# Two weight sums by accumulating transfers, deeper load-ahead, and one more seven-product block in an encoder layer

## The chip, the cores and the metric

The kernel runs on one core of a Trainium2 chip. The metric is device microseconds of one execution; the median of three runs before the change is 883.03 us (882.75 to 883.29). TensorE (PE) multiplies, VectorE (DVE) and ScalarE (ACT) do elementwise work, GpSimd (POOL) does nearly nothing, SyncE (SP) issues nearly all transfers. All arithmetic is float32; each matrix product is made of three TensorE passes over a high and a low part of both operands, so every weight block is first split into two tiles.

## The reference

An encoder layer over 528 tokens (16 learned ones and 512 given) of width 1024: a feed-forward part, a mixer, a second feed-forward part, a last norm. Each feed-forward part is

```
gate, up = split(rms_norm(h) @ w_in)      # 1024 -> 2 x 2816
h = h + 0.5 * (silu(gate) * up) @ w_out   # 2816 -> 1024
```

The mixer runs a gated linear recurrence in both directions on half of the width and a two-dimensional Fourier transform in groups on the other half, norms both, and projects back to 1024. The output drops the first 16 tokens.

## The kernel before

Activations lie feature by partition: 8 tiles of 128 features by 528 (first layer) or 512 tokens (second). The 2816 hidden features are 22 blocks f of 128. For each block the gate and the up projection are needed, each with 8 weight tiles of 128 x 128.

A classic block (`project`, L454) makes gate and up one after the other: 8 weight tiles times three passes times, in the first layer, two halves of 264 tokens, so 48 matmuls for each and 96 for both. A pair block (`pair`, L376) treats gate and up, two halves of the 8 weight tiles and two halves of the tokens as a 2 x 2 by 2 x 2 product and makes seven products of quarter size in place of eight, 7 x 4 x 3 = 84 matmuls of 264 columns (256 in the second layer). It needs sums of weight quarters (`pair_blocks`, `pair_sums`, `pair_differences`, L96 to L128: four VectorE additions in place on the two raw tiles of 512 KB) and sums of quarters of the activations (`sums_of_x`, L289, once per layer, tiles `z` and `xg` with one buffer each, split into `th` and `tl`). In the first layer blocks 0 to 3 are classic (`CLASSIC1`, L28), in the second 0 and 1; all others are pairs.

Blocks go in chunks; the output projection of a chunk ("out" steps, eight per chunk) is interleaved with the next chunk's blocks (`ffn_steps`, L145). The last two products of a pair are made inside the next pair (`interleaved`, L425), then come the activation function and the split of the result (L409 to L421).

Every weight block is a job in one list (`jobs`). A pair is three jobs. `block` (L217) takes the next job and prepares up to `LOOK` = 3 further ones: it loads the raw tile (ring `wraw`, 4 buffers of 512 KB, SP's queue) and splits it by a ScalarE copy and a VectorE subtraction (L87 and L88, L211 and L212) into a ring of 5 pairs of tiles (`wsp`). A load waits until its buffer of the ring is free, and SP issues in order.

Each engine has one queue in order. Its order is written by a list scheduler when the program is built, by the order of the code and by what it holds ready, so an instruction can stand ahead of one that the code has earlier. PSUM has 8 banks in one ring (L72). In the first layer the first three projections (`lead`, L523) hold two banks each until block 0 and 1 are evacuated by `gate_up` (L444), whose tiles `q` and `u` have two buffers each.

Of the kernel before, what the change touches and what calls it, by code (L numbers as in the profile page):

```python
# [9 lines left out]
F32 = mybir.dt.float32  # L10
F32R = mybir.dt.float32r
AF = mybir.ActivationFunctionType
ALU = mybir.AluOpType
# [13 lines left out]
CHUNKS2 = [4, 5, 5, 4, 4]  # L27
CLASSIC1 = {0, 1, 2, 3}  # L28
CLASSIC2 = {0, 1}
# [28 lines left out]

LOOK = 3


@with_exitstack
def encoder_layer(ctx: ExitStack, tc: tile.TileContext, xT, vecs, w1i, w1o, wm, wg, wo, w2i, w2o,
# [29 lines left out]
    def quarter(t, i):  # L93
        return t[:, 512 * i:512 * (i + 1)].rearrange("p (k m) -> p k m", m=P)

    def pair_blocks(pair):  # L96

        raw = []
        for src in pair["src"]:
            r = wraw.tile([P, 1024], F32, tag="raw", name="raw")  # L100
            nc.sync.dma_start(r.rearrange("p (k m) -> p k m", m=P), src)
            raw.append(r)
        pair["raw"] = raw
        hi, lo = w_tiles()
        split_w(hi, lo, raw[0])
        jh = state["pool"].tile([P, 512], F32R, tag="jh", name="jh")
        jl = state["pool"].tile([P, 512], F32R, tag="jl", name="jl")
        split_w(jh, jl, raw[1][:, 512:])
        g, u = raw
        nc.vector.tensor_tensor(g[:, :512], g[:, :512], u[:, :512], op=ALU.subtract)  # L110
        nc.vector.tensor_tensor(u[:, :512], u[:, :512], u[:, 512:], op=ALU.add)
        nc.vector.tensor_tensor(u[:, 512:], u[:, 512:], g[:, :512], op=ALU.subtract)
        return [(quarter(hi, 0), quarter(lo, 0)), (quarter(hi, 1), quarter(lo, 1)), (quarter(jh, 0), quarter(jl, 0))]

    def pair_sums(pair):

        g, u = pair["raw"]
        hi, lo = w_tiles()
        split_w(hi, lo, u)
        nc.vector.tensor_tensor(g[:, 512:], g[:, 512:], u[:, 512:], op=ALU.subtract)  # L120
        return [(quarter(hi, 0), quarter(lo, 0)), (quarter(hi, 1), quarter(lo, 1))]

    def pair_differences(pair):

        g = pair.pop("raw")[0]
        hi, lo = w_tiles()
        split_w(hi, lo, g)
        return [(quarter(hi, 0), quarter(lo, 0)), (quarter(hi, 1), quarter(lo, 1))]  # L128
# [30 lines left out]
    def ffn_jobs(wi, wo_, steps, classic):  # L159
        for kind, f, d in steps:  # L160
            if kind == "out":
                jobs.append((wo_[d][:, f[0]:f[1], :], P, f[1] - f[0], P, 8))
            elif f in classic:
                for b in range(2):
                    jobs.append((wi[f, b], P, 8, P, 2 if len(jobs) < 3 else 8))
            else:
                pair = {"src": (wi[f, 0], wi[f, 1])}
                for part in (pair_blocks, pair_sums, pair_differences):
                    jobs.append((part, pair))
# [14 lines left out]
    ready = {}  # L184
    state = {"load": 0, "next": 0, "use": 0}
    raws = {}

    def load(i):
# [3 lines left out]
        for k in range(0, n, per):  # L192
            e = min(n, k + per)
            yield nc.sync.dma_start(raw[:p, k * m: e * m].rearrange("p (n m) -> p n m", m=m), src[:, k:e, :])

    def prep(i, dest=None):
        if len(jobs[i]) == 2:
            ready[i] = jobs[i][0](jobs[i][1])
            return
        src, p, n, m, per = jobs[i]  # L200
        if i not in raws:
            for _ in load(i):
                pass
# [49 lines left out]
    def vec(name, i=0):  # L253
        return V[:, VOFF[name] + i: VOFF[name] + i + 1]

    hall = xs.tile([P, ND, T], F32, tag="h", name="hall")
    h = [hall[:, d, :] for d in range(ND)]
# [30 lines left out]

    def sums_of_x(g, t0, n, k):  # L289
        m = n // 2  # L290
        a, b = h[k][:, t0:t0 + n], h[k + 4][:, t0:t0 + n]
        xg = tmp.tile([P, HT], F32, tag="xg", bufs=1, name="xg")
        z = tmp.tile([P, 4, HT], F32, tag="z", bufs=1, name="z")
        t1, t2, t3, t4 = [z[:, i, :m] for i in range(4)]
        nc.scalar.activation(xg[:, :m], a[:, :m], AF.Copy, scale=vec(g, k))
        nc.vector.scalar_tensor_tensor(t1, a[:, m:], vec(g, k), xg[:, :m], op0=ALU.mult, op1=ALU.subtract)
        nc.vector.scalar_tensor_tensor(t2, b[:, m:], vec(g, k + 4), t1, op0=ALU.mult, op1=ALU.subtract)
        nc.vector.tensor_tensor(t3, t2, xg[:, :m], op=ALU.subtract)
        nc.vector.scalar_tensor_tensor(t4, b[:, :m], vec(g, k + 4), t2, op0=ALU.mult, op1=ALU.subtract)
        th = xs.tile([P, 8 * QT], F32R, tag=f"th{k}", name=f"th{k}")[:, :4 * HT].rearrange("p (i t) -> p i t", i=4)  # L300
        tl = xs.tile([P, 4, HT], F32R, tag=f"tl{k}", name=f"tl{k}")
        split_to(th[:, :, :m], tl[:, :, :m], z[:, :, :m])
        return th, tl
# [45 lines left out]

    def ffn(X, XT, ss, t0, n, steps, classic, on_done, tail, lead=None):  # L350
        st = {"R": ss} if lead else {}
        half = n // 2
        with tc.tile_pool(name="ffn", bufs=10) as fp, tc.tile_pool(name="ffnt", bufs=2) as ft:
            state["pool"] = ft

            def activated(u):
# [19 lines left out]
            def pair(f, R):  # L376
# [4 lines left out]
                add = ALU.add  # L381
                q = ft.tile([P, 3, HT], F32, tag="q", name="q")
                u = ft.tile([P, 2, HT], F32, tag="u", name="u")
                q0, q1, q2 = [q[:, i, :half] for i in range(3)]
                u0, u1 = [u[:, i, :half] for i in range(2)]
                a11, a12, a22 = block()
# [24 lines left out]
                Rv = like2(R)  # L411
                gv, uv = q[:, :2, :half], u[:, :, :half]
# [49 lines left out]
            for kind, f, d in steps:  # L462
# [20 lines left out]
                else:  # L483
# [50 lines left out]
    for g in preps:  # L534
        next(g, None)
    state["next"] = state["use"] = 3
    W3 = [ready.pop(i) for i in range(3)]
    XT = []
    for k in range(ND):
# [6 lines left out]
    R = rstd_of(q, "r1")  # L546
    for k in range(4):
        XT.append(sums_of_x("g1", 0, T, k))

    ss = new_ss()  # L550
# [5 lines left out]

    ffn(X, XT, R, 0, T, STEPS1, CLASSIC1, done1, None, lead)

# [17 lines left out]

    X2, XT2 = [], []
    ss2 = new_ss()
# [266 lines left out]

    for k in range(4):
        XT2.append(sums_of_x("g2", META, SEQ, k))


    def tail(acts, ft):  # L850
# [21 lines left out]
        def group(t0, t1, between):  # L872
# [24 lines left out]
            for d in (ND - 2, ND - 1):  # L897
                ps = bank("pt")[:, :n]
                project_out(ps, d, t0, t1)
                sq = ft.tile([P, 1, 256], F32, tag="u", name="sqd")[:, :, :n]  # L900
                residual(d, d + 1, t0, t1, ps[:, None, :], sq)
# [37 lines left out]

    ffn(X2, XT2, ss2, META, SEQ, STEPS2, CLASSIC2, None, tail)  # L940

# [82 lines left out]
```

## Time and profile before

| | |
|---|---|
| median of the runs | 883.03 us |
| the profiled execution | 882.88 us |
| its span, first to last instruction | 881.1 us |
| PE busy | 867.3 us (98%), 6410 matmuls |
| DVE busy | 705.7 us (80%) |
| ACT busy | 452.6 us (51%) |
| POOL busy | 0.2 us |
| DMA | 88.14 MB, 100 GB/s in the mean |

The profiled execution's own time is 1.8 us over its span; those lie before the first and after the last instruction shown. Busy shares are means over stages: the first feed-forward layer runs from about 5 to 368 us, the mixer to about 522, the second layer and the output to the end.

### The profile page before, as it was taken

Reading aid. Unit: us, or ns where it says so; the run is one execution under the profiler, and the core shown is the slowest. Engines: PE = TensorE matmul, PEld = TensorE weight load, DVE = VectorE, ACT = ScalarE, POOL = GpSimd, SP = SyncE. Lnnn points to the kernel's source line nnn. Section 1 sums busy time; section 2 is a strip of 40 time slices with the busy share of each in tenths; the row PEclk is TensorE's granted clock in tenths of the full one; section 3 lists DMA queues with packets and bytes.
Section 4 is the critical chain, followed back from the end, with each engine's and each line's share of the span. In section 5 each row is a group of like instructions: output and inputs, shape, how many; then the busy total and the mean of one; then the engine's idle time right before and its main releaser. Section 6 shows DMA issues by size and latency. Waiting matters only on the chain.

```text
span 881.1 us, 15747 instructions
## 1 busy us (share of the span) xinstructions
PE 867.3 (98%) x6410; PEld 826.1 (94%) x6410; DVE 705.7 (80%) x1166; ACT 452.6 (51%) x701; POOL 0.2 (0%) x4
## 2 busy tenths in 40 slices
PE   9999999999999999999989999999999999999996
PEld 8999999999999999999877888999999999989996
DVE  7998776887878876967997689888787887778754
ACT  8744344444444444667837555455454444444444
POOL 0000000000000000000000000000000000000000
PEclk9999999999999999999999999999999999999998
DMA  7422332233243233423323221232433414414212
GB/s 240 151 83 87 110 107 85 85 102 115 73 121 96 76 106 106 137 78 102 118 69 96 87 81 48 84 120 85 126 102 91 128 56 140 114 48 133 73 48 96
DMA packets 33496, 88.14 MB, mean 100 GB/s; under 512 B 3728, under 2 KB 7568, under 8 KB 33424
## 3 DMA queue, kind: packets, MB, share of 16 engines
q1 hardware_dynamic: 32880, 86.62, 32.9%
q8 instruction: 50, 0.82, 0.4%
q10 hardware_dynamic: 544, 0.52, 0.2%
q14 instruction: 22, 0.18, 0.1%
HBM read 85.03 MB, written 2.10 MB: 99 GB/s over the span
## 4 chain that ended last, share of the span: by engine, by line
PE 90%; DVE 5%; ACT 2%; DMA 1%; issue 1%; SPq 1%; DVEq 0%
PE pp L233 15%; PE pp L229 14%; PE pp L231 14%; PE po L231 9%; PE po L233 9%; PE po L229 9%; PE pw L231 2%; PE pw L233 2%; PE pw L229 2%; PE pm L233 1%; PE pm L229 1%; PE pm L231 1%; PE pu L229 1%; PE pu L231 1%; PE pu L233 1%; DMA hall<-in_xT 1%
## 5 line engine op out<-in xcount | busy, mean ns | idle before, releaser
L87 ACT ACTIVATE whi<-raw 128x1024 fp32r<-128x1024 f32 x114 | 120.4, 1061 | 81.9 <-PE po L231 28.1
L88 DVE TENSOR_TENSOR wlo<-raw,whi 128x1024 fp32r<-128x1024 f32 x114 | 139.0, 1222 | 18.1 <-ACT whi L87 17.9
L211 ACT ACTIVATE whi<-raw 128x512 fp32r<-128x512 f32 (+4 forms) x120 | 88.0, 740 | 117.3 <-PE po L231 63.5
L233 PE MATMUL pp<-xh,wlo 128*128 128x256 f32 (+1 forms) x456 | 129.2, 283 | 0.0
L229 PE MATMUL pp<-th,whi 128*128 128x256 f32 (+1 forms) x456 | 129.2, 283 | 0.0
L233 PE MATMUL pp<-th,wlo 128*128 128x256 f32 (+1 forms) x456 | 129.1, 283 | 0.0
L231 PE MATMUL pp<-tl,whi 128*128 128x256 f32 (+1 forms) x456 | 129.0, 283 | 0.0
L231 PE MATMUL pp<-xl,whi 128*128 128x256 f32 (+1 forms) x456 | 128.7, 282 | 0.0
L229 PE MATMUL pp<-xh,whi 128*128 128x256 f32 (+1 forms) x456 | 128.7, 282 | 0.0
L233 PE MATMUL po<-ah,wlo 128*128 128x264 f32 (+1 forms) x496 | 128.5, 317 | 0.0
L231 PE MATMUL po<-al,whi 128*128 128x264 f32 (+1 forms) x496 | 128.5, 317 | 0.0
L229 PE MATMUL po<-ah,whi 128*128 128x264 f32 (+1 forms) x496 | 128.4, 317 | 0.0
L212 DVE TENSOR_TENSOR wlo<-raw,whi 128x512 fp32r<-128x512 f32 (+4 forms) x120 | 98.3, 824 | 10.9 <-ACT whi L211 9.3
L233 PEld LDWEIGHTS po<-ah,wlo 128*128 128x128 f32 x496 | 81.6, 188 | 6.3
L231 PEld LDWEIGHTS po<-al,whi 128*128 128x128 f32 x496 | 81.7, 188 | 5.8
L229 PEld LDWEIGHTS po<-ah,whi 128*128 128x128 f32 x496 | 81.5, 188 | 5.8 <-ACT ah L275 0.2
L229 PEld LDWEIGHTS pp<-xh,whi 128*128 128x128 f32 x456 | 86.0, 189 | 0.9
L231 PEld LDWEIGHTS pp<-xl,whi 128*128 128x128 f32 x456 | 85.8, 188 | 0.9
L233 PEld LDWEIGHTS pp<-th,wlo 128*128 128x128 f32 x456 | 86.0, 189 | 0.0
L229 PEld LDWEIGHTS pp<-th,whi 128*128 128x128 f32 x456 | 85.9, 188 | 0.0
L233 PEld LDWEIGHTS pp<-xh,wlo 128*128 128x128 f32 x456 | 85.8, 188 | 0.0
L231 PEld LDWEIGHTS pp<-tl,whi 128*128 128x128 f32 x456 | 85.8, 188 | 0.0
(218 smaller groups left out, 1736.8 us busy)
## 6 DMA issues: line engine op xcount, KB each, us to landing
raw<-in_w2i SPq DMA_DIRECT2D x44, 512.0 KB, 3.6
raw<-in_w1i SPq DMA_DIRECT2D x41, 512.0 KB, 3.8
raw<-in_w1o SPq DMA_DIRECT2D x32, 256.0 KB, 2.7
raw<-in_wm SPq DMA_DIRECT2D x12, 512.0 KB, 3.8
raw<-in_w2o SPq DMA_DIRECT2D x24, 256.0 KB, 3.0
raw<-in_w2o SPq DMA_DIRECT2D x16, 320.0 KB, 3.1
raw<-in_wo SPq DMA_DIRECT2D x8, 512.0 KB, 3.6
raw<-in_w1o SPq DMA_DIRECT2D x8, 384.0 KB, 3.2
```

The costliest lines, as they stand in the source:

```text
L87: nc.scalar.activation(hi, raw, AF.Copy)
L88: nc.vector.tensor_tensor(lo, raw, hi.bitcast(F32), op=ALU.subtract)
L211: nc.scalar.activation(hi[:p, s], raw[:p, s], AF.Copy)
L212: nc.vector.tensor_tensor(lo[:p, s], raw[:p, s], hi[:p, s].bitcast(F32), op=ALU.subtract)
L229: nc.tensor.matmul(o, wh, xh[i], start=first, stop=False, skip_group_check=go_on)
L231: nc.tensor.matmul(o, wh, xl[i], start=False, stop=False, skip_group_check=go_on)
L233: nc.tensor.matmul(o, wl, xh[i], start=False, stop=last, skip_group_check=go_on)
```

## The change

For each pair three raw buffers are loaded by SP: all of up (a), all of gate (b), and once more the first half of up (c). Two transfers issued by GpSimd then add gate's second half onto b's first half and gate's first half onto c's first half. Two VectorE additions make the other two sums. The names swap: what was gate is now up, and the activations' sums come with their signs turned (a tile `minus` of negated gains), so the gate leaves the products negated and is multiplied by -1 inside the activation function. The order at a pair's end changes with it: now gate takes the last product.

Loads are fetched up to `FETCH` = 6 jobs ahead (splits stay at 3), from a ring of 7 raw buffers in place of 4. `sums_of_x` moves into the feed-forward part and takes its scratch tile from the ring `q` (two buffers, now five quarters wide) that `gate_up` and `pair` use too; `z`, `xg` and `u` go. Block 3 of the first layer becomes a pair. The descriptor scratch of the build goes from 2048 to 1024 bytes.

```diff
-CLASSIC1 = {0, 1, 2, 3}
+CLASSIC1 = {0, 1, 2}
+FETCH = 6
-    wraw = ctx.enter_context(tc.tile_pool(name="wraw", bufs=4))
+    wraw = ctx.enter_context(tc.tile_pool(name="wraw", bufs=7))
+    def pair_loads(pair):
+        up, gate = pair["src"]
+        raw = [wraw.tile([P, 1024], F32, tag="raw", name="raw") for _ in range(3)]
+        a, b, c = [r.rearrange("p (k m) -> p k m", m=P) for r in raw]
+        nc.sync.dma_start(a, up)
+        nc.sync.dma_start(b, gate)
+        nc.sync.dma_start(c[:, :4], up[:, :4])
+        nc.gpsimd.dma_start(b[:, :4], gate[:, 4:], accum_op=ALU.add)
+        nc.gpsimd.dma_start(c[:, :4], gate[:, :4], accum_op=ALU.add)
+        pair["raw"] = raw
     def pair_blocks(pair):
-        split_w(hi, lo, raw[0])
+        split_w(hi, lo, a)
...
-        split_w(jh, jl, raw[1][:, 512:])
-        g, u = raw
-        nc.vector.tensor_tensor(g[:, :512], g[:, :512], u[:, :512], op=ALU.subtract)
-        nc.vector.tensor_tensor(u[:, :512], u[:, :512], u[:, 512:], op=ALU.add)
-        nc.vector.tensor_tensor(u[:, 512:], u[:, 512:], g[:, :512], op=ALU.subtract)
+        split_w(jh, jl, b[:, 512:])
+        nc.vector.tensor_tensor(b[:, 512:], b[:, 512:], c[:, :512], op=ALU.add)
+        nc.vector.tensor_tensor(c[:, 512:], a[:, 512:], b[:, 512:], op=ALU.add)
     def pair_sums(pair):
-        nc.vector.tensor_tensor(g[:, 512:], g[:, 512:], u[:, 512:], op=ALU.subtract)
...
+    def fetch(i):
+        if len(jobs[i]) > 2:
+            if i not in raws:
+                for _ in load(i):
+                    pass
+        elif jobs[i][0] is pair_blocks:
+            pair_loads(jobs[i][1])
     def block(dest=None):
         while state["next"] < min(len(jobs), i + LOOK + 1):
+            while state["fetched"] < min(len(jobs), i + FETCH + 1):
+                fetch(state["fetched"])
+                state["fetched"] += 1
...
-    def sums_of_x(g, t0, n, k):
+    def sums_of_x(pool, g, t0, n, k):
-        xg = tmp.tile([P, HT], F32, tag="xg", bufs=1, name="xg")
-        z = tmp.tile([P, 4, HT], F32, tag="z", bufs=1, name="z")
+        z = pool.tile([P, 5, HT], F32, tag="q", name="z")
...
+        nc.vector.scalar_tensor_tensor(t3, t2, -1.0, xg, op0=ALU.mult, op1=ALU.subtract)
...
     def ffn(...):
             state["pool"] = ft
+            XT = [sums_of_x(ft, g, t0, n, k) for k in range(4)]
...
-                nc.vector.tensor_tensor(q0, q0, R[:, :half], op=ALU.mult)
-                nc.vector.tensor_tensor(q1, A, R[:, half:n], op=ALU.mult)
-                nc.scalar.activation(gv, gv, AF.Silu)
+                uv, gv = q[:, :2, :half], q[:, 3:, :half]
                 nc.vector.tensor_tensor(gv, gv, Rv, op=ALU.mult)
-                nc.vector.tensor_tensor(uv, uv, gv, op=ALU.mult)
+                nc.scalar.activation(gv, gv, AF.Silu, scale=-1.0)
+                nc.vector.tensor_tensor(gv, gv, Rv, op=ALU.mult)
+                nc.vector.tensor_tensor(q0, q0, u0, op=ALU.mult)
+                nc.vector.tensor_tensor(q1, A, u1, op=ALU.mult)
```

## Rows read from the trace of the kernel before

**Rows 1.** the page, part 1: busy us (share) xinstructions, by engine

```profile
PE 867.3 (98%) x6410; PEld 826.1 (94%) x6410; DVE 705.7 (80%) x1166; ACT 452.6 (51%) x701; POOL 0.2 (0%) x4
```

**Rows 2.** windows: stretch, length, busy of PE, PEld, DVE, ACT, POOL, clock, DMA share, GB/s

```profile
24.00:48.00 24.00, 24.00 (x201) 24.00 (x200) 24.00 (x42) 14.76 (x21) 0.00 (x0) 1.00 0.35 111
48.00:72.00 24.00, 24.00 (x200) 24.00 (x199) 20.48 (x34) 11.45 (x17) 0.00 (x0) 1.00 0.26 77
...
250.00:300.00 50.00, 50.00 (x414) 50.00 (x413) 40.55 (x69) 23.86 (x36) 0.00 (x0) 1.00 0.36 101
420.00:470.00 50.00, 45.11 (x314) 40.27 (x312) 46.88 (x79) 31.04 (x52) 0.00 (x0) 1.00 0.31 94
```

**Rows 3.** waits of TensorE and its weight loads: total us, times, longest

```profile
PE py L233 <- DVE a L276: 2.9, 3, 1.7
...
PEld po L229 <- ACT ah L275: 0.2, 1, 0.2
```

**Rows 4.** timeline of TensorE: start us, us, line, op; blocks 2 to 6

```profile
32.47 0.41 PE L229 MATMUL pg<-xh,whi 128*128 128x264 f32 x2
...
44.05 0.40 PE L229 MATMUL pg<-xh,whi 128*128 128x264 f32 x2
...
55.62 0.28 PE L229 MATMUL pp<-xh,whi 128*128 128x264 f32 x1
...
83.36 0.41 PE L229 MATMUL po<-ah,whi 128*128 128x264 f32 x2
```

**Rows 5.** lines: xcount, busy us, mean ns, idle before; VectorE in pairs

```profile
L88 DVE TENSOR_TENSOR wlo<-raw,whi 128x1024 fp32r<-128x1024 f32 x114 | 139.0, 1222 | 18.1 <-ACT whi L87 17.9
...
L120 DVE TENSOR_TENSOR raw<-raw 128x512 f32<-128x512 f32 x38 | 26.1, 687 | 0.3
...
L110 DVE TENSOR_TENSOR raw<-raw 128x512 f32<-128x512 f32 x38 | 26.0, 684 | 0.0
...
L392 DVE TENSOR_TENSOR q<-q,pp 128x256 f32<-128x256 f32 (+1 forms) x38 | 16.1, 424 | 49.0 <-PE pp L233 49.0
```

**Rows 6.** timeline of VectorE, first feed-forward layer's start

```profile
27.70 0.42 DVE L242 TENSOR_TENSOR g<-lead,r 128x264 f32<-128x264 f32 x1
...
44.53 1.26 DVE L276 TENSOR_TENSOR tl<-z,th 128x1056 fp32r<-128x1056 f32 x1
```

**Rows 7.** the tile z: times, ns min/median/max, first and last start in us

```profile
L296 DVE SCALAR_TENSOR_TENSOR z<-hall,V,xg x8: 474/480/491, 20.8 to 539.8; 128x264 f32<-128x264 f32 x4, 128x256 f32<-128x256 f32 x4
```

**Rows 8.** timeline of all engines, end of the last pair of layer one

```profile
343.63 0.65 ACT L415 ACTIVATE q<-q 128x528 f32<-128x528 f32 x1
344.32 0.70 DVE L416 TENSOR_TENSOR q<-q,r 128x528 f32<-128x528 f32 x1
344.94 0.42 DVE L409 TENSOR_TENSOR u<-u,pp 128x264 f32<-128x264 f32 x1
345.40 0.71 DVE L417 TENSOR_TENSOR u<-u,q 128x528 f32<-128x528 f32 x1
346.14 0.64 ACT L275 ACTIVATE ah<-u 128x528 fp32r<-128x528 f32 x1 [1.86 <-DVE u L417]
346.61 0.85 PE L229 MATMUL po<-ah,whi 128*128 128x264 f32 x4
```

**Rows 9.** timeline, start of the second feed-forward layer

```profile
544.91 1.22 DVE L276 TENSOR_TENSOR tl<-z,th 128x1024 fp32r<-128x1024 f32 x1
...
546.65 0.28 PE L229 MATMUL pp<-xh,whi 128*128 128x256 f32 x1
```

**Rows 10.** the page, parts 3 and 6: queue traffic, DMA issues to landing

```profile
q1 hardware_dynamic: 32880, 86.62, 32.9%
...
raw<-in_w1o SPq DMA_DIRECT2D x32, 256.0 KB, 2.7
```

**Rows 11.** timeline of SP's queue, one period of pair and two outs

```profile
226.59 2.21 SPq L101 DMA_DIRECT2D raw<-in_w1i  x2
242.66 2.20 SPq L101 DMA_DIRECT2D raw<-in_w1i  x2
```

More of the change, by code (lines that the diff above doesn't have):

```diff
@@ L94, in quarter @@
         return t[:, 512 * i:512 * (i + 1)].rearrange("p (k m) -> p k m", m=P)
-    def pair_blocks(pair):
[L98 to L103, printed above, removed]
+    def pair_loads(pair):
[8 more added lines that the diff above has]
+        pair["raw"] = raw
+    def pair_blocks(pair):
+        a, b, c = pair["raw"]
         hi, lo = w_tiles()
-        split_w(hi, lo, raw[0])
+        split_w(hi, lo, a)
         jh = state["pool"].tile([P, 512], F32R, tag="jh", name="jh")
         jl = state["pool"].tile([P, 512], F32R, tag="jl", name="jl")
-        split_w(jh, jl, raw[1][:, 512:])
-        g, u = raw
-        nc.vector.tensor_tensor(g[:, :512], g[:, :512], u[:, :512], op=ALU.subtract)
-        nc.vector.tensor_tensor(u[:, :512], u[:, :512], u[:, 512:], op=ALU.add)
-        nc.vector.tensor_tensor(u[:, 512:], u[:, 512:], g[:, :512], op=ALU.subtract)
+        split_w(jh, jl, b[:, 512:])
+        nc.vector.tensor_tensor(b[:, 512:], b[:, 512:], c[:, :512], op=ALU.add)
+        nc.vector.tensor_tensor(c[:, 512:], a[:, 512:], b[:, 512:], op=ALU.add)
         return [(quarter(hi, 0), quarter(lo, 0)), (quarter(hi, 1), quarter(lo, 1)), (quarter(jh, 0), quarter(jl, 0))]
     def pair_sums(pair):
-        g, u = pair["raw"]
         hi, lo = w_tiles()
-        split_w(hi, lo, u)
-        nc.vector.tensor_tensor(g[:, 512:], g[:, 512:], u[:, 512:], op=ALU.subtract)
+        split_w(hi, lo, pair["raw"][1])
         return [(quarter(hi, 0), quarter(lo, 0)), (quarter(hi, 1), quarter(lo, 1))]
     def pair_differences(pair):
-        g = pair.pop("raw")[0]
         hi, lo = w_tiles()
-        split_w(hi, lo, g)
+        split_w(hi, lo, pair.pop("raw")[2])
         return [(quarter(hi, 0), quarter(lo, 0)), (quarter(hi, 1), quarter(lo, 1))]
@@ L166, in ffn_jobs @@
             else:
-                pair = {"src": (wi[f, 0], wi[f, 1])}
+                pair = {"src": (wi[f, 1], wi[f, 0])}
                 for part in (pair_blocks, pair_sums, pair_differences):
@@ L184, in encoder_layer @@
     ready = {}
-    state = {"load": 0, "next": 0, "use": 0}
+    state = {"fetched": 0, "next": 0, "use": 0}
     raws = {}
@@ L200, in prep @@
         src, p, n, m, per = jobs[i]
-        if i not in raws:
-            for _ in load(i):
-                pass
         raw = raws.pop(i)
@@ L254, in vec, with less @@
         return V[:, VOFF[name] + i: VOFF[name] + i + 1]
+    minus = const.tile([P, 24], F32, name="minus")
+    def less(name, i):
+        return minus[:, VOFF[name] + i: VOFF[name] + i + 1]
     hall = xs.tile([P, ND, T], F32, tag="h", name="hall")
@@ L285, in gained @@
         return xh, xl
-    def sums_of_x(g, t0, n, k):
+    def sums_of_x(pool, g, t0, n, k):
         m = n // 2
         a, b = h[k][:, t0:t0 + n], h[k + 4][:, t0:t0 + n]
-        xg = tmp.tile([P, HT], F32, tag="xg", bufs=1, name="xg")
-        z = tmp.tile([P, 4, HT], F32, tag="z", bufs=1, name="z")
[L294 to L299, printed above, removed]
+        z = pool.tile([P, 5, HT], F32, tag="q", name="z")
+        t1, t2, t3, t4, xg = [z[:, i, :m] for i in range(5)]
+        nc.scalar.activation(xg, a[:, :m], AF.Copy, scale=vec(g, k))
+        nc.vector.scalar_tensor_tensor(t1, a[:, m:], less(g, k), xg, op0=ALU.mult, op1=ALU.add)
+        nc.vector.scalar_tensor_tensor(t2, b[:, m:], less(g, k + 4), t1, op0=ALU.mult, op1=ALU.subtract)
+        nc.vector.scalar_tensor_tensor(t3, t2, -1.0, xg, op0=ALU.mult, op1=ALU.subtract)
+        nc.vector.scalar_tensor_tensor(t4, b[:, :m], less(g, k + 4), t2, op0=ALU.mult, op1=ALU.subtract)
         th = xs.tile([P, 8 * QT], F32R, tag=f"th{k}", name=f"th{k}")[:, :4 * HT].rearrange("p (i t) -> p i t", i=4)
         tl = xs.tile([P, 4, HT], F32R, tag=f"tl{k}", name=f"tl{k}")
-        split_to(th[:, :, :m], tl[:, :, :m], z[:, :, :m])
+        split_to(th[:, :, :m], tl[:, :, :m], z[:, :4, :m])
         return th, tl
@@ L347, in new_ss, with ffn @@
         return tmp.tile([P, T], F32, tag="ss", bufs=1, name="ss")
-    def ffn(X, XT, ss, t0, n, steps, classic, on_done, tail, lead=None):
+    def ffn(X, g, ss, t0, n, steps, classic, on_done, tail, lead=None):
         st = {"R": ss} if lead else {}
@@ L381, in pair @@
                 add = ALU.add
[L382 to L385, printed above, removed]
+                q = ft.tile([P, 5, HT], F32, tag="q", name="q")
+                q0, q1, q2, u0, u1 = [q[:, i, :half] for i in range(5)]
                 a11, a12, a22 = block()
@@ L494, in ffn @@
                         on_done(d)
+    nc.vector.tensor_scalar(minus, V[:, :24], -1.0, None, op0=ALU.mult)
     sp4 = const.tile([P, 8], F32, name="sp4")
@@ L535, in encoder_layer @@
         next(g, None)
-    state["next"] = state["use"] = 3
+    state["next"] = state["use"] = state["fetched"] = 3
     W3 = [ready.pop(i) for i in range(3)]
-    XT = []
     for k in range(ND):
@@ L555, in done1 @@
         add_square(ss, h[d], T, d == 0)
-    ffn(X, XT, R, 0, T, STEPS1, CLASSIC1, done1, None, lead)
+    ffn(X, "g1", R, 0, T, STEPS1, CLASSIC1, done1, None, lead)
     wfc = wraw.tile([P, 1024], F32, tag="raw", name="wfc")[:, :NL * P]
@@ L938, in tail @@
             pass
-    ffn(X2, XT2, ss2, META, SEQ, STEPS2, CLASSIC2, None, tail)
+    ffn(X2, "g2", ss2, META, SEQ, STEPS2, CLASSIC2, None, tail)
 def _constants():
```

15 lines of the change are left out of this document (5 added, 10 removed).

## The prediction

> **What bounds the kernel now.** I read the page's first part, then the windows, then TensorE's own waits. TensorE is busy 867.3 of 881.1 us, VectorE 705.7 [rows 1]. The windows say where each counts: in the feed-forward layers TensorE is busy in every microsecond (24.00 of 24, 50.00 of 50) at a granted clock of 1.00, even where VectorE is full as well (24.00 of 24 between 24 and 48 us); only in the mixer does TensorE lose time, 4.9 us between 420 and 470 us, with VectorE at 46.88 of 50 [rows 2]. The waits agree: TensorE's longest wait in total is one of the mixer, 2.9 us on VectorE; in the feed-forward layers its weight loads wait 0.2 us at one place, for the activations after the last pair [rows 3]. So in the two layers the end is set by the number of matmuls. VectorE's time there is worth nothing until it makes TensorE wait.
>
> **The change part by part.**
>
> Block 3 as a pair. From the first matmul of block 3 at 44.05 to that of block 4 at 55.62 lie 96 matmuls in 11.57 us, 0.1205 each. From 55.62 to the first matmul of an output projection at 83.36 lie blocks 4 and 5 with 84 each and five of the seven products of block 6, 60, so 228 in 27.74 us, 0.1217 each [rows 4]. A pair takes 84 x 0.1217 = 10.22 us. Gain: 11.57 - 10.22 = 1.35 us, all of it on the path, since TensorE is full there. This is the one term that surely shortens the end.
>
> Sums on VectorE. Four additions per pair (lines 110, 111, 112 and 120; the rows show the first and the last, 0.684 and 0.687 us) become two [rows 5]: 1.37 us less for a pair, 52 us over 38 pairs. In 250 to 300 us VectorE had 9.4 us to spare already [rows 2], and TensorE waited for none of it: 0 us. I see no bound below that in the layers, as TensorE can't be busier than it is.
>
> VectorE at the start. As a pair, block 3 costs VectorE one more 1024-wide split (1.22), the 512-wide one and two additions (three times 0.69) and three small additions on PSUM (0.42 each), 4.5 us in all [rows 5]; blocks 4 and 5 give back 2.7. Between 24 and 72 us VectorE was busy 44.5 of 48 [rows 2]; it becomes 46.3 of 46.65. That is full. The sums of activations must now be there for block 3's third product, at 44.05 + 24 x 0.1217 = 46.97 [rows 4]; the last one ended at 45.8 [rows 6]. One 1024-wide split fewer (block 3 prepared two before its start, now one) stands against the additions, and two scratch buffers instead of one shorten the chain. I take 0, with bounds 0 and 3 us (one full sum late, below).
>
> Scratch from the ring `q`. A sum of activations is four operations of about 0.48 us [rows 7] and a 1.26 us subtraction [rows 6], 3.2 us of VectorE; four of them now share two buffers with `gate_up`. Before, block 0's evacuation began at 27.70 [rows 6], and it had to, because six of the eight PSUM banks belong to `lead`, two to the running projection, and the next one needs two at 32.47 [rows 4]. If block 0 gets its buffer only after the third sum, it starts at 20.8 [rows 7] + 3 x 3.2 + 1.2 for a weight split that block 1 needs [rows 5] + the fourth sum's first operations 1.9 = 33.5, and the first bank is free at 33.9: a wait of 1.5 us, or 2.8 if the fourth sum's subtraction goes first too. If block 0 is served before the third or fourth sum, it is 0. The order before was no strict program order, VectorE turned to whatever was ready; I take 0 as likelier and keep 1.5 as a rival. In the second layer the same ring is less tight (a projection holds one bank): the sums were done at 546.1, their first use follows two products after 546.65, 24 matmuls of 0.1205 x 256/264 = 0.117 us later, 549.5 [rows 4, 9]. The new place may hold the first sum back until the mixer's tiles are gone, 3.2 us more work behind, against 2.7 us freed in pairs 2 and 3: 0, bounds 0 and 2.
>
> Order at a pair's end. Before, the multiplications by the norm factor and the activation function (0.65 on ScalarE, 0.70) ran ahead of the last addition; behind it came 0.42, 0.71 and 0.64 us until the high part was there, 1.8 us [rows 8]. Now the gate takes the last product: 0.42 + 0.70 + 0.65 + 0.70 + two of 0.42 + 0.64 = 4.0 us, 2.2 longer. TensorE covers it by working on: at 346.61 four matmuls of one kind stand together, the queue mixing the last pair's columns with those of the next output blocks [rows 8]. Inside a layer there are besides two more products of the next pair (2.9 us) in between. There are ten chunk ends; 0 to 2.2 us each. Before, the model behind the order missed by 0.2 [rows 3]; I take 0.4 us in total, twice that.
>
> Loads six ahead, a ring of seven. TensorE waits for no load in the layers [rows 3]; 0. Each pair has three loads on SP in place of two (about 1.1 us each with its wait, two issues in 2.21 us of a period of 16.07 [rows 11]) and two on GpSimd's queue, which has no other work. Traffic: 39 x 0.79 MB = 31 MB on 86.6, so the queue's share of 32.9% [rows 10] becomes some 45%, or 52% if the additions' reads of their targets count too. Not a bound.
>
> The accumulating transfers. None is in the trace. Nearest row: a plain load of 256 KB lands in 2.7 us [rows 10]; I take 2.7 to 5.4, twice, since the target is read too, and nearer the upper. The buffer c of a pair is free when the pair before has its blocks prepared, a period of 16.07 us [rows 11] ahead of the same step of its own; less some 5 us for that preparation and 2.7 for the load, about 8 us are left: hidden, 0 us. Without that cover VectorE, in order, stops at the addition on b, and the evacuations behind it stop too. The Trainium skill (DMA: Bandwidth & Descriptors, section on the anatomy of one DMA) gives a transfer issued by GpSimd about 2 us plus its bytes at 436 GB/s, by my estimate from it 2.6 us here; the sum would be the same by it, and no run here shows it yet.
>
> **Sum.** 882.88 of the profiled execution - 1.35 + 0.4 = 881.9. The median lies 0.15 above that execution: 882.1 us.
>
> **Rivals.** (1) Block 0 waits for the ring `q`, or VectorE, full to 72 us, falls behind: 1.5 us, and up to 4 where a late sum (to 3) adds to it: 882.1 + 1.5 = 883.6. For it: six banks held, the next needed at 32.47, and VectorE with no gap [rows 2, 4]. Against: one buffer less of waiting in the sums, and a queue that takes what is ready. (2) The mixer is dealt anew. Its 4.9 us of idle TensorE hang on the order of VectorE's queue [rows 2, 3], and the splits that stand in that queue will come at other times with other loads ahead; 1.5 us less gives 880.6, 1.5 more or missed chunk ends 883.9. For it: VectorE is at 94% there and three waits of up to 1.7 us make 2.9 of the loss; against: no operation of the mixer is changed. (3) The accumulating transfers land late, the case that ends slower. It decides at about 12 us each: 8 of lead plus the 4.4 us per period that VectorE has free (9.4 x 16.07/50 + 1.4). At 12.6 it is 39 x 0.6 = 23 us: 905. For it: no row shows such a transfer; against: 4.5 times the plain load. The Trainium skill (SBUF — State Buffer, section on who interferes with whom) says a two-port VectorE operation shuts GpSimd out of making descriptors, while a two-input one takes only the read side. If all VectorE work shut it out, as that page does not say, block 3's additions would come after 48 us. No row here bears on it. (4) The relief of VectorE is a gain after all, 52 us of it: excluded by rows 2 as far as the layers go.
>
> **How the numbers follow.** Chances: the forecast 0.40, rival 1 0.28, rival 2 0.16 for the better and 0.10 for the worse half (with the chunk ends), rival 3 0.06. From 883.03 this measurement can tell 0.2%, 1.77 us, so faster means under 881.26 and slower over 884.8. The forecast's 1.35 lies just inside: 0.12 of its 0.40 falls under 881.26 (no loss at chunk ends and a little luck). Faster: 0.12 + 0.15 = 0.27. Slower: rival 1's upper third 0.10, rival 2's 0.05, rival 3's 0.06 = 0.21. Same: 0.52. Range: down to 880.6 less a further 0.7 for both good cases together, 879.9; up to 882.1 + 4 = 886.1; rival 3 and some of the tails are left out.
>
> **What would show it.** Right: matmuls 6398, 12 fewer; TensorE full in the layers; block 3 to 4 in 10.2 us; VectorE's sum near 705.7 - 52 + 4.5 = 658 us; accumulates landing in under 8 us. Wrong: a TensorE gap between 30 and 50 us on `g<-lead` or on `tl<-z`; waits for the high part at chunk ends beyond 0.4 us together; VectorE idle behind a transfer onto `raw`; a changed idle time of TensorE between 420 and 470 us.

## The result and the profile after

The changed kernel is slower: 892.64 us (median of four runs, 890.14 to 892.93) against 883.04, ratio 1.0103, 95% interval 1.0084 to 1.0121. The forecast was 882.1, with a range up to 886.1. A second measurement of the same kernel (experiment 9) gave 892.49 us, ratio 1.0114 (1.0099 to 1.0130). The traced execution is the shortest of the four, 890.14 us with a span of 888.4.

Part 1 of the page and the windows of [rows 2] for the changed kernel, with two more windows at the end (columns as there):

```profile
PE 871.6 (98%) x6398; PEld 828.6 (93%) x6398; DVE 668.3 (75%) x1097; ACT 455.0 (51%) x706; POOL 68.4 (8%) x82
```

```profile
24.00:48.00 24.00, 20.81 (x171) 20.44 (x170) 23.45 (x40) 15.10 (x21) 4.43 (x6) 1.00 0.61 142
48.00:72.00 24.00, 23.84 (x196) 23.63 (x196) 17.88 (x26) 11.30 (x18) 2.37 (x3) 1.00 0.68 163
250.00:300.00 50.00, 49.99 (x411) 49.77 (x410) 36.83 (x61) 22.71 (x34) 5.24 (x6) 1.00 0.60 148
420.00:470.00 50.00, 46.43 (x327) 42.62 (x326) 45.60 (x76) 30.81 (x53) 0.00 (x0) 0.97 0.27 89
862.00:866.00 4.00, 3.08 (x27) 2.88 (x26) 2.34 (x5) 3.57 (x8) 0.00 (x0) 1.00 0.00 0
866.00:870.00 4.00, 4.00 (x22) 4.00 (x23) 0.17 (x1) 1.68 (x5) 0.00 (x0) 0.57 0.00 0
```

TensorE has 12 matmuls fewer, as costed, and VectorE's busy time fell by 37 us against [rows 1]; the kernel is slower all the same. Against [rows 2] TensorE lost 3.2 of 24 us at the start, where it had lost nothing. At the end it pauses, and then runs four microseconds at a mean granted clock of 0.57: 22 matmuls where 36 fit at full clock (a window of four microseconds of the kernel before is shown with experiment 9).

The waits of TensorE and its weight loads (total, times, longest) say for whom. They answer to [rows 3]:

```profile
PE pg L242 <- DVE q L255: 2.9, 1, 2.9
PE py L246 <- DVE a L295: 2.1, 2, 1.7
...
PE sums L892 <- ACT sqd L882: 0.9, 1, 0.9
```

```profile
PEld po L242 <- ACT ah L294: 2.6, 9, 0.8
```

Two new things: one wait of 2.9 us at the start on VectorE's evacuation of `lead` (line 255), and the wait for the activations' high part at chunk ends, 0.2 us once in [rows 3], now 2.6 us at nine of the ten chunk ends. The mixer's wait (`py`) did not grow.

Where the difference arises, read from the start times of the matmuls in the traces (us; the last row gives the stretches in which TensorE's granted clock was at the lower of its two levels, 1.2 GHz, the one at an execution's very end left out):

| | before | after | 9: after, again | 2: one scratch | 3: gate first | 12: both |
|---|---|---|---|---|---|---|
| first matmul of block 2 | 32.47 | 35.26 | 35.92 | 32.94 | 35.75 | 33.31 |
| from there to the mixer's first | 335.53 | 337.20 | 338.66 | 337.51 | 335.93 | 334.68 |
| the mixer, to block 0 of layer two | 154.67 | 154.38 | 154.39 | 154.34 | 154.38 | 154.36 |
| layer two, block 0 to the last product | 323.79 | 324.17 | 324.14 | 323.96 | 323.02 | 322.85 |
| from the last product to the span's end | 34.65 | 37.35 | 35.78 | 37.32 | 34.46 | 34.45 |
| lower clock | none | 446.6 to 450.0, 866.4 to 869.8 | 36.9 to 40.3, 449.9 to 453.3 | 445.0 to 448.4, 864.8 to 868.3 | 35.4 to 38.8 | 443.5 to 446.9 |

The losses sit in the first, second and fifth rows, and the two repairs (experiments 2 and 3) take them away separately. The second row hides a loss behind a gain: with 1.35 us fewer matmuls it should have fallen to 334.2.

**The start.** VectorE's timeline of the changed kernel, where block 0 waits to be evacuated, and TensorE's answer:

```profile
25.09 1.26 DVE L295 TENSOR_TENSOR tl<-z,th 128x1056 fp32r<-128x1056 f32 x1 [0.33 <-ACT th L294]
...
28.20 1.25 DVE L295 TENSOR_TENSOR tl<-z,th 128x1056 fp32r<-128x1056 f32 x1
...
33.20 1.25 DVE L295 TENSOR_TENSOR tl<-z,th 128x1056 fp32r<-128x1056 f32 x1
34.37 0.49 DVE L315 SCALAR_TENSOR_TENSOR z<-hall,minus,z 128x264 f32<-128x264 f32 x1
34.77 0.43 DVE L255 TENSOR_TENSOR q<-lead,r 128x264 f32<-128x264 f32 x1
```

```profile
35.26 0.39 PE L242 MATMUL pg<-xh,whi 128*128 128x264 f32 x1 [2.86 <-DVE q L255]
```

The evacuation that began at 27.70 in [rows 6] begins at 34.77, behind the third sum's subtraction. That is rival 1 of the prediction, which put it at 33.5.

**A pair's end.** VectorE and ScalarE behind the last pair's last product, the answer to [rows 8] (in the second layer, ahead of the tail):

```profile
849.53 2.50 DVE L222 TENSOR_TENSOR taill<-raw,tailh 128x512 fp32r<-128x512 f32 x4 [0.32 <-ACT tailh L221]
851.94 0.41 DVE L426 TENSOR_TENSOR q<-q,pp 128x256 f32<-128x256 f32 x1
852.39 0.69 DVE L430 TENSOR_TENSOR q<-q,r 128x512 f32<-128x512 f32 x1
853.11 0.63 ACT L431 ACTIVATE q<-q 128x512 f32<-128x512 f32 x1 [2.05 <-DVE q L430]
853.78 0.69 DVE L432 TENSOR_TENSOR q<-q,r 128x512 f32<-128x512 f32 x1 [0.70 <-ACT q L431]
854.51 0.43 DVE L433 TENSOR_TENSOR q<-q 128x256 f32<-128x256 f32 x1
854.85 0.41 DVE L434 TENSOR_TENSOR q<-pp,q 128x256 f32<-128x256 f32 x1
855.30 0.63 ACT L294 ACTIVATE ah<-q 128x512 fp32r<-128x512 f32 x1 [1.55 <-DVE q L434]
```

From the last addition (851.94) to the high part's end (855.93) is 4.0 us, the prediction's figure to the tenth. At the same place the kernel before took 2.9 us, with one split of the tail's weights in between:

```profile
847.10 0.42 DVE L409 TENSOR_TENSOR u<-u,pp 128x256 f32<-128x256 f32 x1
849.36 0.63 ACT L275 ACTIVATE ah<-u 128x512 fp32r<-128x512 f32 x1 [2.34 <-DVE u L417]
```

The tail's TensorE catches up with the longer chain and stops for 0.1 us (its weight load for 0.3), and later stops again at the sums:

```profile
864.01 0.61 PE L892 MATMUL sums<-ones,sqd 128*128 128x1 f32 x4 [0.92 <-ACT sqd L882]
```

### The profile page after: what moved, and what is told of

It reads as the page before. It is cut to its first block, busy times and chain, and to the rows that moved or that the text cites. A ratio compares the mean times of both kernels' runs of the same rounds, so it can differ in the third digit from the quotient of the medians.

```text
span 888.4 us, 16061 instructions
## 1 busy us (share of the span) xinstructions
PE 871.6 (98%) x6398; PEld 828.6 (93%) x6398; DVE 668.3 (75%) x1097; ACT 455.0 (51%) x706; POOL 68.4 (8%) x82
## 3 DMA queue, kind: packets, MB, share of 16 engines
q1 hardware_dynamic: 38496, 96.84, 35.2%
q0 software_dynamic: 11232, 20.45, 14.6%
## 5 line engine op out<-in xcount | busy, mean ns | idle before, releaser
L89 DVE TENSOR_TENSOR wlo<-raw,whi 128x1024 fp32r<-128x1024 f32 x117 | 142.8, 1221 | 33.2 <-ACT whi L88 33.1
L88 ACT ACTIVATE whi<-raw 128x1024 fp32r<-128x1024 f32 x117 | 123.6, 1060 | 73.8 <-PE pp L244 38.7
L221 ACT ACTIVATE whi<-raw 128x512 fp32r<-128x512 f32 (+4 forms) x118 | 85.6, 734 | 105.9 <-PE po L244 55.2
L242 PE MATMUL pp<-th,whi 128*128 128x256 f32 (+1 forms) x468 | 132.8, 284 | 0.2 <-ACT q L406 0.2
L246 PE MATMUL pp<-xh,wlo 128*128 128x256 f32 (+1 forms) x468 | 132.4, 283 | 0.0
L246 PE MATMUL pp<-th,wlo 128*128 128x256 f32 (+1 forms) x468 | 132.1, 282 | 0.0
L242 PE MATMUL pp<-xh,whi 128*128 128x256 f32 (+1 forms) x468 | 132.1, 282 | 0.0
L244 PE MATMUL pp<-xl,whi 128*128 128x256 f32 (+1 forms) x468 | 132.0, 282 | 0.0
L244 PE MATMUL pp<-tl,whi 128*128 128x256 f32 (+1 forms) x468 | 131.9, 282 | 0.0
L222 DVE TENSOR_TENSOR wlo<-raw,whi 128x512 fp32r<-128x512 f32 (+4 forms) x118 | 96.0, 818 | 14.1 <-ACT whi L221 13.1
```

The costliest lines, as they stand in the source:

```text
L88: nc.scalar.activation(hi, raw, AF.Copy)
L89: nc.vector.tensor_tensor(lo, raw, hi.bitcast(F32), op=ALU.subtract)
L242: nc.tensor.matmul(o, wh, xh[i], start=first, stop=False, skip_group_check=go_on)
L244: nc.tensor.matmul(o, wh, xl[i], start=False, stop=False, skip_group_check=go_on)
L246: nc.tensor.matmul(o, wl, xh[i], start=False, stop=last, skip_group_check=go_on)
```

## The experiments

The numbers in the texts on record count the kernels in this order; ratios are against the kernel before, run beside them.

**1. The sums' scratch off the ring, many buffers.**

```diff
-        z = pool.tile([P, 5, HT], F32, tag="q", name="z")
+        z1 = pool.tile([P, T], F32, tag="ah", name="z1")...   # pool: the ring of 10
+        z2 = pool.tile([P, T], F32, tag="al", name="z2")...
+        xg = tmp.tile([P, T], F32, tag="sq", bufs=2, name="xg")[:, :m]
```

> The changed kernel, with the scratch of the activations' sums taken out of the ring q: each sum has two buffers of its own (in the ring of ten that the activations use later) and nothing waits for a buffer. The two 528-wide subtractions in place of one 1056-wide cost some 0.1 us per sum. Theory 1 (block 0's evacuation waits for a buffer of the shared ring): the gap of TensorE at 32.1 us, 3.0 us, goes; 892.64 - 2.9 = 889.7 us. Theory 2 (not the buffer, but the order in VectorE's queue: the sums come first in the code, and with several buffers nothing makes the builder turn to the evacuation in between, as the single scratch buffer did before): the gap stays or grows, since four sums instead of three can go ahead; 892.6 to 896 us, TensorE's gap at 32 us 3 to 6 us.

896.07 us (895.18 to 896.94), ratio 1.0152 (1.0138 to 1.0166). The gap stays: block 0's evacuation begins behind seven of the eight half subtractions.

```profile
34.19 0.70 DVE L295 TENSOR_TENSOR tl<-z,th 128x528 fp32r<-128x528 f32 x1
34.80 0.43 DVE L255 TENSOR_TENSOR q<-lead,r 128x264 f32<-128x264 f32 x1
```

So taking the shared buffer away alone does not close the gap (2.5 us is left of 2.9): theory 2 holds, and theory 1 (rival 1 as it was worded) falls as the whole cause. In the second layer the same thing costs more: the norm factor's chain waits 3.3 us behind the sums (TensorE, `psn`, from 540.9 to 544.2 us), and the kernel is 3.4 us slower than the changed one.

**2. One scratch for all four sums.**

```diff
+            z1 = fp.tile([P, T], F32, tag="ah", name="z1")...
+            z2 = fp.tile([P, T], F32, tag="al", name="z2")...
+            xg = tmp.tile([P, T], F32, tag="sq", bufs=2, name="xg")
+            XT = [sums_of_x((z1, z2, xg), g, t0, n, k) for k in range(4)]
```

> As the first, but all four sums use one and the same scratch of their own, so each must wait for the subtraction of the sum before, as in the kernel before. Theory 1 and theory 2 both: the gap at 32.1 us goes, 892.64 - 2.9 = 889.7 us. A rival, that VectorE's work as such is too much for the start (block 3 as a pair adds 4.5 us): the gap moves to the next projection or to the first product with a sum, near 47 us, and the time falls by less than 1 us, 892 us.

886.60 us (885.26 to 887.84), ratio 1.0043 (1.0031 to 1.0056). The gap is gone; each sum now waits for the subtraction before it, and the builder puts evacuations into these waits:

```profile
26.94 0.70 DVE L295 TENSOR_TENSOR tl<-z,th 128x528 fp32r<-128x528 f32 x1
27.56 0.42 DVE L255 TENSOR_TENSOR q<-lead,r 128x264 f32<-128x264 f32 x1
28.33 0.71 DVE L295 TENSOR_TENSOR tl<-z,th 128x528 fp32r<-128x528 f32 x1 [0.34 <-ACT th L294]
```

By the medians it gained 6.0 us, twice the gap: theory and rival both missed the size. The two traces, both with a low-clock stretch in the tail and none at the start, lie only 2.3 us apart (spans 888.4 and 886.1); the rest is taken up below.

**3. Gate first at a pair's end.**

```diff
-                pair = {"src": (wi[f, 1], wi[f, 0])}
+                pair = {"src": (wi[f, 0], wi[f, 1])}
...
+                gv, uv = q[:, :2, :half], q[:, 3:, :half]
+                nc.vector.tensor_tensor(q0, q0, R[:, :half], op=ALU.mult)
+                nc.vector.tensor_tensor(q1, A, R[:, half:n], op=ALU.mult)
+                nc.scalar.activation(gv, gv, AF.Silu)
+                nc.vector.scalar_tensor_tensor(gv, gv, -1.0, Rv, op0=ALU.mult, op1=ALU.mult)
+                nc.vector.tensor_tensor(uv, uv, gv, op=ALU.mult)
```

> The changed kernel with the roles of gate and up swapped back: up takes the last product, its sign is turned in the multiplication behind the activation function, and gate is complete earlier. Theory A (the chain behind a pair's last product is 2.2 us longer and shows at chunk ends and in the tail): TensorE's gaps at the four chunk ends of layer one after the first (0.2 to 0.3 us each, two instructions) and at 89 us (0.9) shrink, some 1.5 to 2 us, and the tail's late start and its idle 1.1 us near 862.8 us shrink by 1 to 3 us, with the low clock behind it (3.4 us at half, 1.7 us of work) gone or not; together 887 to 890 us. Rival B (these gaps come from VectorE's order alone): no more than 0.5 us, 892 us. The gap at 32.1 us stays at 3 us by either.

885.14 us (883.77 to 887.09), ratio 1.0029 (1.0020 to 1.0038): 7.5 us gained, more than theory A's 2.6 to 5.6; rival B falls. The gap at 32 us stayed, at 2.9 us. The high part follows the last addition by 2.9 us, with one split of the tail in between, and no wait for it at a chunk end of layer one is left in the list:

```profile
849.74 0.41 DVE L426 TENSOR_TENSOR q<-q,pp 128x256 f32<-128x256 f32 x1
850.07 0.68 DVE L433 SCALAR_TENSOR_TENSOR q<-q,r 128x512 f32<-128x512 f32 x1
850.67 0.68 DVE L222 TENSOR_TENSOR taill<-raw,tailh 128x512 fp32r<-128x512 f32 x1
851.27 0.69 DVE L434 TENSOR_TENSOR q<-q 128x512 f32<-128x512 f32 x1
851.99 0.63 ACT L294 ACTIVATE ah<-q 128x512 fp32r<-128x512 f32 x1 [2.34 <-DVE q L434]
```

**4 and 12. Both.** Edits 2 and 3 together, run twice.

> The second and the third together. If the two causes are separate and are all there is, the gains add: 892.64 - 2.9 - (2.5 to 5.6) = 884 to 887 us; if they account for everything the forecast's terms are left, 881.7 us. If the accumulating transfers, the load-ahead or the mixer carry a part of the loss, it stays above 885 us with gaps of TensorE elsewhere.

> The fourth kernel once more, to settle whether it is faster than the kernel before: there it took 881.88 us against 882.75, a ratio of 0.9992 with an interval that just reaches 1. If the forecast's sum holds once both causes are gone (881.7 us by its two terms), the same again, 881.9 us. If that was chance, 882.7 us. A trace of an execution without the low clock at 24 us should show a start as in the kernel before (second block's first matmul near 32.9 us) and a span near 880 us.

881.88 us (881.01 to 884.20), ratio 0.9992 (0.9983 to 1.0001), and 881.37 us (880.90 to 884.18), ratio 0.9987 (0.9977 to 0.9996). With both causes gone the time is that of the forecast's own sum, 881.9, and in the second measurement the version is faster than the kernel before by 0.13%. The sum fits better than its parts, and that is in part luck: in this trace the start is 0.8 us later than in the kernel before, layer one gains 0.85 us and not 1.35, and the mixer, layer two and the tail give 0.3, 0.9 and 0.2 that no term forecast. Block 2 started at 33.31 (expected near 32.9), and the span was 879.7. TensorE's list of waits has neither of the two new ones.

**5. Both, and all four sums of a pair on VectorE.**

```diff
-        nc.sync.dma_start(c[:, :4], up[:, :4])
-        nc.gpsimd.dma_start(b[:, :4], gate[:, 4:], accum_op=ALU.add)
-        nc.gpsimd.dma_start(c[:, :4], gate[:, :4], accum_op=ALU.add)
...
+        nc.vector.tensor_tensor(c[:, :512], a[:, :512], b[:, :512], op=ALU.add)
+        nc.vector.tensor_tensor(b[:, :512], b[:, :512], b[:, 512:], op=ALU.add)
```

> The fourth kernel (one scratch, gate first) without the accumulating transfers: VectorE makes all four sums of a pair again, two additions of 0.69 us more for each of 39 pairs, 53 us of VectorE; 78 transfers on GpSimd's queue and 39 loads of 256 KB go. Ring and load-ahead stay. Theory (the relief of VectorE and the transfers are both off the path, as the prediction costed them): the same time, 881.9 us (881.0 to 882.8). Rival 1 (the relief is a gain of its own: the second layer took 299.1 us from its last classic matmul to its last product where the kernel before took 300.0): 0.9 us slower or more, 882.8 to 885 us. Rival 2 (the transfers hold something up): faster, under 881 us.

882.86 us (882.29 to 884.68), ratio 1.0003 (0.9994 to 1.0012), 1.0 and 1.5 us above the two medians of the version with the transfers. Rival 1 of this experiment: the relief of VectorE is worth something (net of whatever the transfers cost, as both went together), but not in layer two (322.99 there, against 322.85). It is worth 0.9 to 1.3 us in layer one (from block 2's first matmul to the mixer 335.98, against 335.04 and 334.68 in the traces of experiments 4 and 12), where VectorE is nearly full to 72 us. The same window for this kernel and for the version with the transfers (experiment 12):

```profile
48.00:72.00 24.00, 23.82 (x193) 23.39 (x193) 23.47 (x38) 12.06 (x19) 0.00 (x0) 1.00 0.37 118
```

```profile
48.00:72.00 24.00, 24.00 (x198) 23.95 (x197) 22.31 (x38) 12.98 (x22) 2.77 (x4) 1.00 0.70 175
```

**6. Both, with block 3 classic** (`CLASSIC1 = {0, 1, 2, 3}`).

> The fourth kernel with block 3 classic again, 96 matmuls instead of 84. Theory (the one term that surely shortens the end): 1.35 us slower, 881.88 + 1.35 = 883.2 us. Rival (VectorE is so full at the start that the pair's 4.5 us there eat the gain): the same or faster, 881 to 882 us.

882.67 us (882.20 to 883.20), ratio 0.9999 (0.9990 to 1.0008): 0.8 and 1.3 us above the two medians with the pair. From block 2 to the mixer it takes 335.90, against 335.04 and 334.68: 0.9 to 1.2 of the 1.35.

**7. The kernel before with gate last, alone.**

```diff
-                pair = {"src": (wi[f, 0], wi[f, 1])}
+                pair = {"src": (wi[f, 1], wi[f, 0])}
...
+                nc.vector.tensor_tensor(gv, gv, Rv, op=ALU.mult)
+                nc.scalar.activation(gv, gv, AF.Silu)
+                nc.vector.tensor_tensor(gv, gv, Rv, op=ALU.mult)
+                nc.vector.tensor_tensor(q0, q0, u0, op=ALU.mult)
+                nc.vector.tensor_tensor(q1, A, u1, op=ALU.mult)
```

> The kernel before with one thing alone: gate and up change places in a pair, so that gate takes the last product. Nothing else differs, no transfer, ring or sum. Theory A (the longer chain at a pair's end is a cause by itself): slower by what the fourth kernel gained over the second, 886.60 - 881.88 = 4.7 us, so 887.5 us (886.5 to 889), with gaps of 0.2 to 1 us at the chunk ends of layer one and 1.1 us idle ahead of the sums in the tail. Rival (it hurts only together with other parts of the change): under 884 us.

889.01 us (888.86 to 892.11), ratio 1.0080 (1.0067 to 1.0092). The order at a pair's end costs 6.2 us with nothing else changed: theory A, at the upper end of its range. Read as in the table, it is 2.4 us in layer one, 0.6 in layer two and 2.9 in the tail (337.88, 324.36, 37.52). The traced execution is the longest of the five, 892.11; the clock stood at its lower level from 24.7 to 31.5 us in it, before block 2. The order leaves the same two marks:

```profile
PEld po L229 <- ACT ah L275: 2.5, 8, 0.6
PEld sums L880 <- ACT sqd L870: 1.1, 1, 1.1
```

**8. The kernel before with block 3 as a pair, alone** (`CLASSIC1 = {0, 1, 2}`).

> The kernel before with block 3 as a pair, alone. Theory: 12 matmuls fewer, 882.75 - 1.35 = 881.4 us. Rival (with four additions per pair VectorE, 24.00 of 24 us busy there, falls behind at the start and TensorE waits): 882.8 us or more, with a gap between 30 and 60 us.

882.92 us (882.61 to 884.46), ratio 1.0004 (0.9995 to 1.0013). Twelve matmuls fewer and no gain: from block 2 to the mixer it takes 335.76 us where 334.2 were due. VectorE, with four additions per pair, is nearly full, and TensorE has lost 0.27 us in this window, more at other places up to 87 us. Experiment 5, with the same four additions but the ring of seven and the deeper load-ahead, loses there too, which speaks against the loads as the reason.

```profile
48.00:72.00 24.00, 23.73 (x194) 23.44 (x194) 23.59 (x37) 12.84 (x20) 0.00 (x0) 1.00 0.38 120
```

**9. The changed kernel again.**

> The changed kernel once more, unaltered, for its spread: of four executions one took 890.14 and three 892.6 to 892.9 us, and the one with a trace is the first. The two causes found so far add to 881.88 + (886.60 - 881.88) + (885.14 - 881.88) = 889.9 us, which is that one; the other three are 2.7 us longer. Theory: in these TensorE's clock falls to its lower level after the 3.0 us gap at 32 us, as it did at 35.4 us in the first and the third kernel's traces (3.41 us long, 1.7 us of work), and perhaps once more; most executions then lie near 892 us and a trace of one has such a stretch between 30 and 40 us. Rival: a third cause that the traced execution does not have; then the trace has TensorE idle at another place.

892.49 us (890.67 to 894.93). The traced execution (890.67) had the stretch that the theory wanted; its windows, and after them the same two of the kernel before:

```profile
32.00:36.00 4.00, 1.15 (x10) 0.94 (x9) 4.00 (x8) 1.09 (x1) 1.11 (x2) 1.00 0.77 189
36.00:40.00 4.00, 4.00 (x22) 4.00 (x23) 3.87 (x9) 3.01 (x3) 0.00 (x0) 0.61 0.47 79
```

```profile
32.00:36.00 4.00, 4.00 (x36) 4.00 (x35) 4.00 (x9) 2.36 (x4) 0.00 (x0) 1.00 0.45 131
36.00:40.00 4.00, 4.00 (x36) 4.00 (x35) 4.00 (x8) 1.79 (x3) 0.00 (x0) 1.00 0.20 27
```

The gap is followed by a stretch at the lower level (1.2 GHz), 22 matmuls instead of 36. So the theory's stretch is there, but in an execution as short as the first trace's: alone it does not make the longer ones. This execution had none in the tail, and the first trace had one there and none here. No trace shows both.

**10 and 11. Gate first, sums on the shared ring, but written behind block 0's or block 1's evacuation.**

```diff
-            XT = [sums_of_x(ft, g, t0, n, k) for k in range(4)]
+            XT = []
...
                     acts[f] = gate_up(*ps)
+                    if f == 0:        # experiment 11: f == 1
+                        XT += [sums_of_x(ft, g, t0, n, k) for k in range(4)]
```

> Gate first, and the sums back on the shared ring q with its two buffers, but written in the code behind block 0's evacuation instead of ahead of it. Theory (what counts is where the evacuation stands in VectorE's queue, and that follows from the order of the code when the sums have several buffers): no gap at 32 us, as the fourth kernel, 881.9 us (880.9 to 883). Rival (sharing the ring is harmful by itself): block 1's evacuation waits for the third sum's buffer and a gap of 1 to 3 us opens between 36 and 48 us: 883 to 885 us.

> The same with the sums behind block 1's evacuation. The two evacuations come first in any case; the last sum's subtraction then stands behind that of block 2's gate in VectorE's queue. Theory: block 3's third product, near 47 us, waits for the late sums, 1 to 3 us: 883 to 885 us. Rival (VectorE's order adapts, everything is in time): 881 to 882 us, the best version.

883.25 us (882.36 to 885.25), ratio 1.0008 (0.9999 to 1.0017), and 893.10 us (890.83 to 894.99), ratio 1.0118 (1.0102 to 1.0135). In both the gap at 32 us is gone with the ring still shared (block 2 starts at 32.61 and 33.39): block 0's evacuation follows its place in the code. In the tenth, block 1's takes its place in the queue: VectorE begins it at 43.11, right behind the second and third sums' subtractions, the third being the one whose buffer it takes over. Block 1's split and ScalarE's work behind it are late, and TensorE stops at block 3's third product, for a copy that ScalarE has queued behind them:

```profile
40.36 2.43 DVE L295 TENSOR_TENSOR tl<-z,th 128x1056 fp32r<-128x1056 f32 x2
42.70 0.50 DVE L314 SCALAR_TENSOR_TENSOR z<-hall,minus,z 128x264 f32<-128x264 f32 x1
43.11 0.43 DVE L255 TENSOR_TENSOR q<-lead,r 128x264 f32<-128x264 f32 x1
```

```profile
50.59 0.39 PE L242 MATMUL pp<-th,whi 128*128 128x264 f32 x1 [1.64 <-ACT q L406]
```

That is the rival's mechanism, and its time at the lower end, with the gap 2 us later than it said: sharing the ring does harm as well. It is read from this trace; a run with the sums at this place in the code and a scratch of their own, which would part the two, was not made.

In the eleventh the sums come too late in both layers, worst in the second (block 0 to the last product 329.1 us, against 322.85): theory's side, but 8 us more than it said, since it priced layer one alone.

## Why the prediction was wrong

**The step that failed first** is the order at a pair's end: "I take 0.4 us in total". The chain itself was right (4.0 us, 2.2 longer); its cover was not. The argument was that TensorE mixes the last pair's columns with later work and that earlier waits were 0.2 us. But the queue had only just enough of such work for the shorter chain; the list behind [rows 3] had a second wait of 0.2 us of this kind, at the tail, that the prediction passed over:

```profile
PEld pt L229 <- ACT ah L275: 0.2, 1, 0.2
```

Experiment 7 prices the step at 6.2 us alone, experiments 2 and 4 at 4.7 inside the changed kernel. By the table (2 against 12) it is 2.8 us in layer one, 1.1 in layer two, 2.9 in the tail (6.8 together; the two traced executions lie 6.4 apart, the medians of experiments 2 and 4 only 4.7). Of the tail's 2.9, 1.6 is the low-clock stretch behind its wait: the changed kernel's tail took 37.35 us with it and 35.78 without. The tail had no term of its own in the sum: "ten chunk ends" counted the end of the layer as one more, though there VectorE also has the tail's weight splits in the same queue (four of them, 2.50 us, stand ahead of the addition in the rows above). Missed chunk ends stood only in the worse half of rival 2, at 883.9.

**The second step** is the scratch ring, where I took "0 as likelier" on the ground that VectorE "turned to whatever was ready". It had turned to block 0 because the single scratch left the next sum waiting: experiment 2 restores that. With more buffers two things put an evacuation behind the sums, the order of the code (experiment 1, no shared ring) and the ring's turn (experiment 10, the code's order mended), and taking away either alone isn't enough. TensorE stood 2.9 us and not rival 1's 1.5; by experiments 3 and 4 the price is 3.3.

Added up, 881.88 + 4.72 + 3.26 = 889.9 us, near the shorter executions of the changed kernel (890.14 and 890.67). The medians lie 2.6 to 2.8 above, so the two do not simply add: repaired first, the ring gives 6.0 us and the order 7.5 (experiments 2 and 3); repaired second, 3.3 and 4.7.

The clock explains a part of that. A low-clock stretch costs 1.5 us in layer one (338.66 against 337.20) and 1.6 in the tail, and each of the two traces of the changed kernel has one of the two. An execution with both would take some 891.6 to 892.2 us by this estimate, still short of the medians. The mean granted clock of the executions agrees: it is 0.993 in the two traced ones and 0.9917, in the mean, in the other six, some 1.2 us of full clock less in 890, while these six take 2.6 us longer. So the clock can be about half of the difference; where the rest comes from stays open.

**Block 3** was sized about right (0.9 to 1.2 of 1.35 in experiment 6) but "surely" was wrong: without the relief of VectorE it is worth nothing (experiment 8). That is also why rival 4 was excluded too quickly. The windows between 250 and 300 us excluded it there; between 24 and 72, where VectorE is nearly full, the relief is worth 1.0 to 1.5 us by the medians (experiment 5). The relief itself was costed right: the durations of VectorE's instructions add up to 775.9 us before and 728.5 after, 47.4 less, where the prediction had 52 - 4.5. But one instruction can begin before the last has ended (34.37 in the rows of the start, where the one before ends at 34.45), and busy time counts the overlap once; so it fell by 37 us, to 668.3 and not to 658.

**Right:** the transfers. They land in 4.0 to 4.5 us in the median, inside the bounds 2.7 to 5.4 (the six issued before 50 us took 5.8), and GpSimd's and SP's queues hold 14.6 and 35.2% of the engines, 49.8 together, for the 45 to 52 forecast:

```profile
q1 hardware_dynamic: 38496, 96.84, 35.2%
q0 software_dynamic: 11232, 20.45, 14.6%
...
raw<-in_w2i POOLq DMA_DIRECT2D x40, 256.0 KB, 4.5
raw<-in_w1i POOLq DMA_DIRECT2D x38, 256.0 KB, 4.0
```

VectorE stood 3.1 us in all for them, ahead of the first addition; the list of TensorE's waits has none for a transfer:

```profile
L118 DVE TENSOR_TENSOR raw<-raw 128x512 f32<-128x512 f32 x39 | 26.8, 688 | 3.7 <-DMA raw<-in_w2i 2.2 <-DMA raw<-in_w1i 0.9
```

The estimate of 2.6 us from the Trainium skill (DMA: Bandwidth & Descriptors, the anatomy of one DMA) is too low for this kind of transfer; the measurement decides. Nor did a busy VectorE shut GpSimd out, the case weighed beside rival 3, which the Trainium skill (SBUF — State Buffer, who interferes with whom) states for two-port operations alone: six issues went out between 24 and 48 us with VectorE at 23.45 of 24. The mixer stayed as it was (154.38 us against 154.67), within the 1.5 us of rival 2.

Left open: layer two takes 0.9 us less in the best version than in the kernel before (322.85 against 323.79), spread over pairs and output projections, and still does with the sums on VectorE (322.99). The deeper load-ahead and the larger ring were never run alone; TensorE's lists have no wait for a load, but that they are worth nothing is not shown.

## What to carry to other kernels

When operands change roles, follow the chain behind the last product operation by operation at every place where nothing follows it, the last block above all; that the engine was covered before says only that the old chain fitted. A scratch with a single buffer can be what holds a queue's order together: before giving it more, ask which instruction goes ahead of which once it no longer waits. A full side engine takes the gain of fewer matmuls, so read its share in the very stretch where the edit lies.

## What the runs showed of the hardware

A short gap of TensorE can cost twice. After the gap of 2.9 us the granted clock stood at its lower level from 36.9 to 40.3 us in one trace of the changed kernel and stayed at 1.00 in the other; after the 0.92 us wait in the tail it was the other way round (866.4 to 869.8). The trace with the stretch took 1.5 us longer in layer one, and 1.6 in the tail. Experiment 1, whose TensorE waited 3.3 us until 544.2, had one more from 544.1 to 547.5. In the mixer, whose operations no kernel here changes, the traces of all but the kernel before and experiment 3 had such a stretch near 445 us (clock 0.97 between 420 and 470 us in the changed kernel, 1.00 in [rows 2]). There it cost nothing: the mixer took 154.38 us with it (the changed kernel) and without it (experiment 3).

Of the 6.0 us that the repair of a 2.9 us gap brought (experiment 2), the traces show 2.3 for the gap and, in an execution that has the stretch, 1.5 for the clock. The rest is not shown.
